# Dense SwiGLU: two thirds of the gate and up blocks as 2 by 2 block products with seven multiplications

## The chip, the core and the metric

The kernel runs on one core of a Trainium2 chip. The metric is the device time of one execution in microseconds. TensorE multiplies (PE in the profile; PEld is its weight load), VectorE (DVE), ScalarE (ACT) and GpSimd (POOL) do elementwise work, and SyncE (SP) issues nearly all of the transfers from device memory. Each engine works through its own instructions in a fixed order.

## The reference

The program is a two-layer encoder trunk on 512 tokens of width 1024. The part that matters here is the dense feed-forward stage at the end of the first layer:

```python
def swiglu(h, wg, wu, wd):
    return (jax.nn.silu(h @ wg) * (h @ wu)) @ wd
# h = rms_norm(x, norm_ffn[l]) is 512 x 1024; wg, wu are 1024 x 2816; wd is 2816 x 1024
x = x + swiglu(h, ffn_wg[j], ffn_wu[j], ffn_wd[j])
```

All of it is float32. The second layer has a mixture of experts in this place, which the change does not touch.

## The kernel before

Each float32 operand is split into two float16 parts, a high part and a low rest, and a product takes three float16 passes: high by high, low by high, high by low (`passes`). An activation is stored transposed, as eight tiles of 128 rows by 512 tokens for each part (`fh`, `fl`).

`ffn` first normalises x and transposes it (`norm_T`), row tile by row tile. Then it walks over 22 column blocks f of 128 columns. For each block it needs gate and up, so two weight blocks of 1024 x 128. `wtile` loads a block (`raw`, 512 KB), ACT writes the high part (`whi`, L266) and DVE the low part (`wlo`, L271). `proj_feat` then makes 24 matmuls of 512 columns into one PSUM bank (`pf`, L289). The first block goes through `proj_first` (L301), which takes the tokens in two halves of 256 columns so that it can start before all four row tiles are normalised. After gate and up, ACT applies silu, DVE multiplies, and the result is split into `uh` and `ul`. At the end `resid` multiplies by `wd` (L331) and adds to x.

Weight tiles come from a pool with two `raw`, three `whi` and three `wlo` buffers; a load is issued by SP when its buffer is free, and SP issues in a fixed order. PSUM gives the stage four banks for products (`acc`) and four for transposes (`sm`). A scheduler fixes the order of each engine's instructions when the program is built. The first weight blocks are loaded and split long before the stage, during the memory attention.

Of the kernel before, what the change touches and what calls it, by code (L numbers as in the profile page):

```python
# [8 lines left out]
F32 = mybir.dt.float32  # L9
# [18 lines left out]
SW = 64.0  # L28
# [26 lines left out]
class Kern:  # L55
# [151 lines left out]
    @staticmethod  # L207
    def plain(t):
        return t.bitcast(F32) if t.dtype == F32R else t
# [1035 lines left out]
            output(1, 1)  # L1245


    def ffn(self, l, x):
        nc, I, tc = self.nc, self.I, self.tc
        hh = self.hp.tile([P, KT, SEQ], F16, name="fh", tag="hh", bufs=1)  # L1250
        hl = self.hp.tile([P, KT, SEQ], F16, name="fl", tag="hl", bufs=1)
        self.norm_T(x, NT, [(I["norm_ffn"][l], hh, hl)])
        j = l // 2
        FT = 22
        hk, lk = [hh[:, k, :] for k in range(KT)], [hl[:, k, :] for k in range(KT)]
        with tc.tile_pool(name="ffn", bufs=1, reuse_waits="tile") as fp:
            uh = fp.tile([P, FT, SEQ], F16, name="uh")
            ul = fp.tile([P, FT, SEQ], F16, name="ul")
            for f in range(FT):
                fs = slice(f * P, (f + 1) * P)  # L1260
                ws = [I["ffn_wg"][j][:, fs], I["ffn_wu"][j][:, fs]]
                if f == 0:
                    pg, pu = self.proj_first(ws, hk, lk)
                else:
                    pg, pu = (self.proj_feat(w, hk, lk) for w in ws)
                s = fp.tile([P, SEQ], F32, name="fs", bufs=2)
                nc.scalar.activation(s, pg, AF.Silu, scale=1 / SW)
                nc.vector.scalar_tensor_tensor(s, pu, 0.125 / SW, s, OP.mult, OP.mult)
                self.split_ps(uh[:, f, :], ul[:, f, :], s)
# [535 lines left out]
```

## Time and profile before

| | us |
|---|---|
| median of 3 runs (2078.53 to 2082.65) | 2080.55 |
| the profiled execution | 2075.39 |
| its span, from first to last instruction | 2073.6 |
| first product of the stage to its last gate or up product | 664.8 to 896.4 |
| `wd` products of the stage | 896.4 to 1008.8 |

In the profile, "busy" is the time in which an engine had an instruction in work, and a row of the chain of waits is a piece of the work that ended last. Matmuls are pipelined: the length of one record is longer than the distance to the next, so the rate is read from a run of many.

### The profile page before, as it was taken

To read this page: it belongs to the slowest core of one execution; us is meant where nothing else is said; L and a number is where in the kernel's file an instruction comes from. 1 tells how busy PE (TensorE), PEld (TensorE's weight loads), DVE (VectorE), ACT (ScalarE), POOL (GpSimd) and SP (SyncE) were. 2 spreads that over 40 slices of the span, in tenths; PEclk is the share of its full clock that TensorE was granted. 3 is DMA by queue.
4 is the path that set the end of the run, shared out by engine and by line. 5 is a ranking of instruction groups with operands and counts; after the bars stand their busy time and mean duration, and the time that the engine had idled before them with its cause. 6 is when DMAs were issued, how large, how long until landed. Compare 5 with 4: busy or idle time off the path is not lost.

```text
span 2073.6 us, 40817 instructions
## 1 busy us (share of the span) xinstructions
PE 1940.1 (94%) x16760; PEld 1286.0 (62%) x16760; DVE 1413.4 (68%) x2373; ACT 1029.1 (50%) x1661; POOL 341.0 (16%) x357
## 2 busy tenths in 40 slices
PE   6998899899898999999998989979998899999997
PEld 3764565465465444444574546537455799999996
DVE  6766987756676333322466998574757888888886
ACT  5543446453453333322443435544335678888883
POOL 2260611003010000000243260100201310000002
PEclk9998999979999999999999999988999899999998
DMA  7334334325642333333434342434535699999993
GB/s 234 106 80 99 87 90 127 97 64 159 221 147 62 102 102 102 102 102 102 121 81 94 89 120 65 120 99 130 173 114 202 189 394 365 356 355 347 345 344 127
DMA packets 346742, 332.52 MB, mean 160 GB/s; under 512 B 101921, under 2 KB 263841, under 8 KB 346546
## 3 DMA queue, kind: packets, MB, share of 16 engines
q1 hardware_dynamic: 335440, 306.03, 47.2%
q10 hardware_dynamic: 8482, 15.39, 2.0%
q0 software_dynamic: 2624, 8.40, 1.2%
q8 instruction: 133, 2.18, 0.4%
q14 instruction: 63, 0.52, 0.1%
HBM read 297.05 MB, written 32.72 MB: 159 GB/s over the span
## 4 chain that ended last, share of the span: by engine, by line
PE 70%; DVE 12%; DMA 7%; ACT 3%; issue 3%; POOL 3%; SPq 2%; DVEq 0%; ACTq 0%; POOLq 0%
PE pf L289 23%; PE ptok L331 12%; PE pe L1567 10%; PE py L1612 6%; PE pSy L904 3%; PE pf L301 3%; PE ptok L349 2%; PE psc L527 1%; DVE wlo L271 1%; DMA eraw<-in_moe_wd_dram 1%; DVE iacc L518 1%; DVE pr L1003 1%; PE pA L808 1%; PE pT L193 1%; PE pp L558 1%
## 5 line engine op out<-in xcount | busy, mean ns | idle before, releaser
L266 ACT ACTIVATE whi<-raw 128x1024 f16<-128x1024 f32 (+2 forms) x244 | 227.7, 934 | 436.9 <-PE pf L289 187.3
L271 DVE SCALAR_TENSOR_TENSOR wlo<-raw,whi 128x1024 f16<-128x1024 f32 (+2 forms) x210 | 232.0, 1107 | 201.7 <-ACT whi L266 190.3
L1550 DVE SCALAR_TENSOR_TENSOR ewlo<-eraw,ewhi 128x1024 f16<-128x1024 f32 x265 | 321.1, 1220 | 58.0 <-ACT ewhi L1549 56.7
L289 PEld LDWEIGHTS <-whi 128*128 128x128 f16 x1888 | 182.5, 99 | 229.5 <-issue 34.8
L1549 ACT ACTIVATE ewhi<-eraw 128x1024 f16<-128x1024 f32 x265 | 277.4, 1054 | 77.9 <-PE py L1612 34.6
L1567 PE MATMUL pe<-XT,ewhi 128*128 128x144 f16 x2816 | 206.3, 226 | 1.7 <-issue 1.7
L1567 PEld LDWEIGHTS <-ewhi 128*128 128x128 f16 x2816 | 183.4, 98 | 2.3 <-issue 1.6
L289 PE MATMUL pf<-hh,whi 128*128 128x512 f16 x448 | 171.7, 383 | 2.6 <-DVE v L613 1.0
L289 PE MATMUL pf<-hl,whi 128*128 128x512 f16 x448 | 171.5, 383 | 0.0
L289 PEld LDWEIGHTS <-wlo 128*128 128x128 f16 x944 | 92.4, 99 | 112.0 <-issue 9.0
L269 POOL TENSOR_TENSOR wlo<-raw,whi 128x1024 f16<-128x1024 f32 (+3 forms) x34 | 59.9, 1761 | 596.1 <-ACT raw L268 512.9
L289 PE MATMUL pf<-fh,whi 128*128 128x512 f16 x336 | 127.3, 379 | 0.0
L289 PE MATMUL pf<-fl,whi 128*128 128x512 f16 x336 | 127.3, 379 | 0.0
L1567 PE MATMUL pe<-XT,ewlo 128*128 128x144 f16 x1408 | 117.2, 226 | 0.1
L289 PE MATMUL pf<-hh,wlo 128*128 128x512 f16 x448 | 112.6, 386 | 0.0
L1612 PE MATMUL py<-HT,ewhi 128*128 128x144 f16 x1408 | 103.9, 227 | 0.1
L1567 PEld LDWEIGHTS <-ewlo 128*128 128x128 f16 x1408 | 94.3, 98 | 0.8 <-issue 0.7
L1612 PEld LDWEIGHTS <-ewhi 128*128 128x128 f16 x1408 | 92.5, 98 | 0.3 <-issue 0.2
L289 PE MATMUL pf<-fh,wlo 128*128 128x512 f16 x336 | 79.4, 379 | 0.0
L349 PE MATMUL ptok<-whi,hh 128*128 128x256 f16 (+1 forms) x320 | 74.7, 274 | 2.1 <-ACT qe L485 2.0
L349 PE MATMUL ptok<-whi,hl 128*128 128x256 f16 (+1 forms) x320 | 75.0, 274 | 0.0
L349 PEld LDWEIGHTS <-hh 128*128 128x128 f16 x640 | 62.4, 100 | 15.5 <-issue 8.2
(462 smaller groups left out, 3879.3 us busy)
## 6 DMA issues: line engine op xcount, KB each, us to landing
raw<-in_w_in_dram SPq DMA_DIRECT2D x76, 512.0 KB, 4.0
eraw<-in_moe_wg_dram SPq DMA_DIRECT2D x16, 2048.0 KB, 12.9
eraw<-in_moe_wu_dram SPq DMA_DIRECT2D x16, 2048.0 KB, 14.3
eraw<-in_moe_wd_dram SPq DMA_DIRECT2D x16, 2048.0 KB, 12.9
eraw<-in_moe_wg_dram SPq DMA_DIRECT2D x8, 1536.0 KB, 11.9
eraw<-in_moe_wu_dram SPq DMA_DIRECT2D x8, 1536.0 KB, 14.6
eraw<-in_moe_wd_dram SPq DMA_DIRECT2D x8, 1536.0 KB, 8.5
raw<-in_ffn_wg_dram SPq DMA_DIRECT2D x22, 512.0 KB
```

The lines of the kernel that those rows point to most:

```text
L266: nc.scalar.activation(hi, raw, AF.Copy, scale=SW)
L269: nc.gpsimd.tensor_tensor(lo, raw, hi, OP.subtract)
L271: nc.vector.scalar_tensor_tensor(lo, raw, SW, hi, OP.mult, OP.subtract)
L289: self.nc.tensor.matmul(p, lhsT=w[:, k, :], rhs=x[k], start=first, stop=last)
L301: m = self.nc.tensor.matmul(ps[i][:, cs], lhsT=w[:, k, :], rhs=x[k][:, cs], start=hf == 0 and start, stop=stop, skip_group_check=True)
L331: mm(ps[t][:, :N], lhsT=x[:, k0 + k, ts], rhs=w[:, k, :], start=k0 == 0 and first, stop=k0 + kg == kt and last)
L349: mm(p, lhsT=x[:, k0 + k, ts], rhs=w[:, k, :], start=k0 == 0 and t % 2 == 0 and first, stop=k0 + kg == kt and last, skip_group_check=True)
L904: m = mm(p[e][:, cc % 4, jj, :], lhsT=l, rhs=r, start=first[e] is None, stop=x == (1 if cc else 0), skip_group_check=True)
L1549: a = nc.scalar.activation(r[0], w, AF.Copy, scale=SW)
L1550: d = nc.vector.scalar_tensor_tensor(r[1], w, SW, r[0], OP.mult, OP.subtract)
L1567: mm(p[:, i * n:(i + 1) * n], lhsT=w[:, k, :], rhs=XT[:, k, h, :], start=z == 0, stop=z == len(ms) - 1)
L1612: mm(ps[d], lhsT=w[:, i, d * P:(d + 1) * P], rhs=HT[:, k, h, :], start=k == 0 and w is wh and h == 0 and d % per == 0, stop=k == FT - 1 an ...
```

## The change

Fourteen of the 22 blocks (all f that are not divisible by 3) are computed by `seven`. There gate and up together are one product of a 512 x 1024 by a 1024 x 256 matrix, seen as 2 by 2 blocks: two halves of the tokens, two halves of the 1024 rows, and gate and up as the two column halves. The Winograd form needs seven block products where the plain way needs eight. Each block product is 12 matmuls of 256 columns.

For this, sums of the activation blocks (S1 to S4) are formed once, in `sums_seven`, from the normalised row tiles, transposed and split. Sums of the weight blocks (T1 to T4, in `sTa` and `sTb`) are formed for each f by four subtractions on POOL. ACT and DVE split B11 with B21, B22, T1 with T2, and T3 with T4 into high and low parts. The results are combined by three copies on ACT and four additions on DVE. Both gate and up of such a block are loaded into a new tile `sraw` (two buffers). The pairs of `sTa` and `sTb` have one buffer each, the split parts two. f = 0, 3, 6, ... 21 stay plain and keep the old weight pool.

```diff
-        self.norm_T(x, NT, [(I["norm_ffn"][l], hh, hl)])
...
+            with tc.tile_pool(name="ffns", bufs=1, side="right", reuse_waits="tile") as sp:
+                xs = self.norm_T(x, NT, [(I["norm_ffn"][l], hh, hl)], None, sp)
+                plain(0, *self.proj_first(blocks(0), hk, lk))
+                self.sums_seven(sp, [t.rearrange("p (a b) -> p a b", a=2) for t in xs], ops)
+            with tc.tile_pool(name="ffn", bufs=2, reuse_waits="tile") as fp:
+                for f in range(1, FT):
+                    if f % 3:
+                        self.seven(fp, *blocks(f), ops, uh[:, f, :], ul[:, f, :])
+                    else:
+                        plain(f, *[self.proj_feat(w, hk, lk) for w in blocks(f)])
...
+    def seven(self, fp, wg, wu, ops, uh, ul):
...
+        raw = fp.tile([P, KT, 256], F32, name="sraw")
+        for i, w in enumerate((wg, wu)):
+            nc.sync.dma_start(raw[:, :, i * P:(i + 1) * P], w.rearrange("(k p) c -> p k c", p=P))
...
+        sub(Ta[:, 0], B(0, 1), B(0, 0))
+        sub(Tb[:, 0], B(1, 1), B(0, 1))
+        sub(Ta[:, 1], B(1, 1), Ta[:, 0])
+        sub(Tb[:, 1], B(1, 0), Ta[:, 1])
...
+            nc.scalar.activation(hi, src, AF.Copy, scale=SW)
+            nc.vector.scalar_tensor_tensor(lo, src, SW, hi, OP.mult, OP.subtract)
...
+        prod(a, 0, "A11", "B11")
+        nc.scalar.copy(p1, a[:, 0])
+        prod(a, 1, "A12", "B21")
+        prod(b, 0, "S3", "T3")
+        nc.scalar.copy(p7, b[:, 0])
+        prod(b, 1, "S1", "T1")
+        nc.vector.tensor_tensor(v, b[:, 1], p7, OP.add)
+        nc.vector.tensor_tensor(R[:, 0], a[:, 1], p1, OP.add)
+        prod(a, 0, "S2", "T2", True)
+        nc.scalar.copy(u2, a[:, 0])
+        nc.vector.tensor_tensor(R[:, 3], a[:, 0], v, OP.add)
+        prod(b, 0, "A22", "T4", True)
+        prod(b, 1, "S4", "B22", True)
+        nc.vector.tensor_tensor(R[:, 1:3], b, u2[:, None, :].to_broadcast([P, 2, 256]), OP.add)
```

The new order on SP, before and after the change, at the start of the stage. Before, the loads that follow the gain vector `gb0` are, one by one, the remaining plain blocks (up of f = 2, gate of f = 3, and on):

```order
L247 DMA gb0_9105<-in_norm_mix_dram 128x1024
L259 DMA raw_7092<-in_ffn_wu_dram 128x8x128
L259 DMA raw_7128<-in_ffn_wg_dram 128x8x128
L259 DMA raw_7159<-in_ffn_wu_dram 128x8x128
L259 DMA raw_7195<-in_ffn_wg_dram 128x8x128
```

After the change, the loads that were issued early belong to f = 0, f = 3 and the gate of f = 6. Behind `gb0` come the up of f = 6 (`raw_7691`) and the gate of f = 9 (`raw_7983`), and only then the four loads of f = 1 (`sraw_7081`) and f = 2 (`sraw_7209`):

```order
L247 DMA gb0_6803<-in_norm_ffn_dram 128x1024
L259 DMA raw_7691<-in_ffn_wu_dram 128x8x128
L259 DMA raw_7983<-in_ffn_wg_dram 128x8x128
L1305 DMA sraw_7081<-in_ffn_wg_dram 128x8x128
L1305 DMA sraw_7081<-in_ffn_wu_dram 128x8x128
L1305 DMA sraw_7209<-in_ffn_wg_dram 128x8x128
L1305 DMA sraw_7209<-in_ffn_wu_dram 128x8x128
```

So f = 1 and f = 2, which the old order had loaded before the stage, now stand behind two loads of later blocks.

The order on ACT, at the same place, after the change. `whi_7662` is the high part of the gate of f = 6; `sB11h`, `sB22h`, `sT1h` and `sT3h` are the high parts for f = 1 (7090 to 7102) and f = 2 (7218, 7222); `sp1_7108` is the copy of the first block product of f = 1:

```order
L266 ACTIVATE whi_7662<-raw_7660 128x1024
L201 CAST s3h_6793<-pT_7034 128x4x128
L201 CAST uh_6795<-fs_7000 128x512
...
L1318 ACTIVATE sB11h_7090<-sraw_7081 128x1024
L1318 ACTIVATE sB22h_7094<-sraw_7081 128x512
L1318 ACTIVATE sB11h_7218<-sraw_7209 128x1024
L1339 COPY sp1_7108<-pf_7106 128x256
L1318 ACTIVATE sB22h_7222<-sraw_7209 128x512
L1318 ACTIVATE sT1h_7098<-sTa_7084 128x1024
L1318 ACTIVATE sT3h_7102<-sTb_7085 128x1024
```

The copy and the splits of T1 and T3 for f = 1 have moved behind work that needs the loads of f = 2. The program makes the second product of f = 1 wait for that copy, since both are in one PSUM bank.

The order on DVE there, after the change (`wlo_7663` is the low part of the gate of f = 6, which frees the buffer for `raw_7983`; the rows ending in l are the low parts of f = 1 and f = 2):

```order
L271 SCALAR_TENSOR_TENSOR wlo_7663<-raw_7660,whi_7662 128x1024
...
L1319 SCALAR_TENSOR_TENSOR sB11l_7091<-sraw_7081,sB11h_7090 128x1024
L1319 SCALAR_TENSOR_TENSOR sB22l_7095<-sraw_7081,sB22h_7094 128x512
L1319 SCALAR_TENSOR_TENSOR sB11l_7219<-sraw_7209,sB11h_7218 128x1024
L1319 SCALAR_TENSOR_TENSOR sB22l_7223<-sraw_7209,sB22h_7222 128x512
L1319 SCALAR_TENSOR_TENSOR sT1l_7099<-sTa_7084,sT1h_7098 128x1024
```

Each of these has two operands in SBUF, and POOL makes the four subtractions of f = 1 in the same stretch.

## Rows read from the trace of the kernel before

**Rows 1.** Page, part 1: engine, busy us, share of span, instructions.

```profile
PE 1940.1 (94%) x16760; PEld 1286.0 (62%) x16760; DVE 1413.4 (68%) x2373; ACT 1029.1 (50%) x1661; POOL 341.0 (16%) x357
```

**Rows 2.** Windows: busy time of each engine, granted clock, DMA share, GB/s.

```profile
660.00:682.00 22.00, 19.89 (x146) 15.34 (x145) 12.62 (x18) 10.02 (x16) 1.66 (x3) 0.92 0.08 26
682.00:720.00 38.00, 38.00 (x177) 17.21 (x176) 14.13 (x16) 13.44 (x17) 0.00 (x0) 1.00 0.43 124
...
1700.00:1750.00 50.00, 50.00 (x786) 49.82 (x784) 42.61 (x44) 40.20 (x50) 2.44 (x2) 1.00 1.02 381
```

**Rows 3.** Chain of waits in order of time: start, length, work.

```profile
670.20 0.87 PE pT L193 x8
...
677.64 3.27 PE pf L301 x30
680.91 215.62 PE pf L289 x999
896.53 112.25 PE ptok L331 x520
```

**Rows 4.** Groups of instructions, 682 to 895 us: busy, mean ns, idle before.

```profile
L271 DVE SCALAR_TENSOR_TENSOR wlo<-raw,whi 128x1024 f16<-128x1024 f32 x42 | 51.2, 1220 | 56.7 <-ACT whi L266 56.7
L266 ACT ACTIVATE whi<-raw 128x1024 f16<-128x1024 f32 x43 | 45.4, 1056 | 102.0 <-PE pf L289 100.1 <-DMA raw<-in_ffn_wu_dram 1.9
...
L202 DVE TENSOR_TENSOR ul<-fs,uh 128x512 f16<-128x512 f32 x21 | 14.4, 685 | 0.0
L201 ACT CAST uh<-fs 128x512 f16<-128x512 f32 x21 | 13.0, 619 | 28.3 <-DVE fs L1268 28.3
```

**Rows 5.** Timeline, 679.5 to 684 us: start, length, engine, instruction.

```profile
679.53 1.22 DVE L271 SCALAR_TENSOR_TENSOR wlo<-raw,whi 128x1024 f16<-128x1024 f32 x1 [4.98 <-ACT whi L266]
...
679.88 1.04 PE L301 MATMUL pf<-fh,wlo 128*128 128x256 f16 x8
...
681.30 1.05 ACT L266 ACTIVATE whi<-raw 128x1024 f16<-128x1024 f32 x1
...
682.38 1.22 DVE L271 SCALAR_TENSOR_TENSOR wlo<-raw,whi 128x1024 f16<-128x1024 f32 x1 [0.26 <-ACT whi L266]
...
683.63 0.38 SPq L259 DMA_DIRECT2D raw<-in_ffn_wg_dram  x1
```

**Rows 6.** Transfer issues: tile, queue, count, size, us to landing.

```profile
raw<-in_ffn_wu_dram SPq DMA_DIRECT2D x22, 512.0 KB, 3.8
```

**Rows 7.** Groups of instructions on POOL, whole span.

```profile
L1075 POOL TENSOR_TENSOR mf<-mf,tb 128x512 f32<-128x512 f32 x16 | 23.7, 1488 | 28.7 <-DVE tb L1074 28.7
...
L269 POOL TENSOR_TENSOR wlo<-raw,whi 128x512 f16<-128x512 f32 x4 | 4.6, 1154 | 5.9 <-ACT raw L268 5.9
```

**Rows 8.** Timeline, two places where DVE and POOL meet.

```profile
485.31 0.69 DVE L271 SCALAR_TENSOR_TENSOR wlo<-raw,whi 128x512 f16<-128x512 f32 x1
485.47 1.65 POOL L1075 TENSOR_TENSOR mf<-mf,tb 128x512 f32<-128x512 f32 x1 [6.16 <-DVE tb L1074]
...
496.67 1.15 POOL L269 TENSOR_TENSOR wlo<-raw,whi 128x512 f16<-128x512 f32 x1
496.74 1.64 DVE L936 TENSOR_TENSOR yc<-yc,var 128x512 f32<-128x512 f32 x1 [1.17 <-POOL var L165]
```

**Rows 9.** Groups of instructions with 256 elements, DVE and ACT.

```profile
L271 DVE SCALAR_TENSOR_TENSOR wlo<-raw,whi 128x256 f16<-128x256 f32 x24 | 10.8, 452 | 1.1 <-ACT whi L266 0.8
...
L869 ACT COPY H<-pH 128x256 f32<-128x256 f32 x16 | 5.2, 375 | 6.1 <-PE pH L866 6.0
```

**Rows 10.** Timeline, 665.9 to 667.5 us: matmuls of 256 columns.

```profile
665.95 0.42 PE L301 MATMUL pf<-fl,whi 128*128 128x256 f16 x1
666.16 0.42 PE L301 MATMUL pf<-fh,whi 128*128 128x256 f16 x1
...
667.09 0.27 PE L301 MATMUL pf<-fl,whi 128*128 128x256 f16 x1
667.20 0.27 PE L301 MATMUL pf<-fh,whi 128*128 128x256 f16 x1
```

More of the change, by code (lines that the diff above doesn't have):

```diff
@@ L1255, in ffn @@
         hk, lk = [hh[:, k, :] for k in range(KT)], [hl[:, k, :] for k in range(KT)]
[L1256 to L1269, printed above, removed]
-            self.resid(I["ffn_wd"][j], uh, ul, x, FT, 8.0)
+        ops = {n: tuple(h[:, 4 * q:4 * q + 4, i * 256:(i + 1) * 256] for h in (hh, hl))
+               for n, i, q in (("A11", 0, 0), ("A12", 0, 1), ("A22", 1, 1))}
@@ new lines, in ffn, with plain @@
+        with tc.tile_pool(name="ffnx", bufs=1, reuse_waits="tile") as xp:
+            for i in range(4):
+                ops[f"S{i + 1}"] = tuple(xp.tile([P, 4, 256], F16, name=f"s{i}{c}") for c in "hl")
+            uh = xp.tile([P, FT, SEQ], F16, name="uh")
+            ul = xp.tile([P, FT, SEQ], F16, name="ul")
+            blocks = lambda f: [I[w][j][:, f * P:(f + 1) * P] for w in ("ffn_wg", "ffn_wu")]
+            def plain(f, pg, pu):
+                t = xp.tile([P, SEQ], F32, name="fs", bufs=2)
+                nc.scalar.activation(t, pg, AF.Silu, scale=1 / SW)
+                nc.vector.scalar_tensor_tensor(t, pu, 0.125 / SW, t, OP.mult, OP.mult)
+                self.split_ps(uh[:, f, :], ul[:, f, :], t)
+            with tc.tile_pool(name="ffns", bufs=1, side="right", reuse_waits="tile") as sp:
[8 more added lines that the diff above has]
+                        plain(f, *[self.proj_feat(w, hk, lk) for w in blocks(f)])
+            self.resid(I["ffn_wd"][j], uh, ul, x, FT, 8.0)
@@ new lines, in sums_seven @@
+    def sums_seven(self, sp, xs, ops):
+        nc = self.nc
+        for tt in range(2):
+            x0, x1 = xs[tt], xs[2 + tt]
+            S = [sp.tile([P, 512], F32, name=f"S{i}") for i in range(4)]
+            nc.gpsimd.tensor_tensor(S[2], x0[:, 0, :], x1[:, 0, :], OP.subtract)
+            nc.vector.tensor_tensor(S[0], x1[:, 0, :], x1[:, 1, :], OP.add)
+            nc.vector.tensor_tensor(S[1], S[0], x0[:, 0, :], OP.subtract)
+            nc.vector.tensor_tensor(S[3], x0[:, 1, :], S[1], OP.subtract)
+            for i in (2, 0, 1, 3):
+                p = self.sm("pT")
+                for k in range(4):
+                    nc.tensor.transpose(p[:, k * P:(k + 1) * P], S[i][:, k * P:(k + 1) * P], self.ident)
+                self.split_ps(*[o[:, :, tt * P:(tt + 1) * P] for o in ops[f"S{i + 1}"]], p.rearrange("p (k t) -> p k t", k=4))
```

29 lines of the change are left out of this document (added).

## The prediction

> **What bounds the kernel now.** I read part 1 of the page first: PE is busy for 94% of the span, DVE for 68%, POOL for 16% [rows 1]. That is an average, so I cut the windows to the stage that changes. From 682 us on PE is busy for all of its 38 us, at full granted clock, while DVE is busy for 14.1 us, ACT for 13.4 and POOL for nothing [rows 2]. The chain of waits says the same more strictly: from 680.91 us there are 215.62 us of nothing but gate and up products, 999 matmuls, and the `wd` products follow at 896.53 without a break [rows 3]. So here the stage lasts as long as its matmuls, 215.62/999 = 0.2158 us for one of 512 columns. A plain block has 48 of them: 10.36 us. Every other engine only has to keep up.
>
> **What the seven products save.** A block by `seven` has 7 x 12 = 84 matmuls of 256 columns. The first block of the stage already runs in such halves: 30 of them take 3.27 us of the chain, 0.109 each, each with its own weight load [rows 3]. So a block costs 84 x 0.109 = 9.16 us and saves 1.20. Fourteen blocks save **16.8 us**, if PE never waits. (Were the price 0.125 instead, 84 of them would cost 10.5 us and the saving would be gone; the 30 in a row say it is not.)
>
> **What is added on PE before the stage flows.** The sums S1 to S4 need 8 groups of 4 transposes. Eight transposes take 0.87 us [rows 3], so a group takes 0.43. In the new order three groups stand before the last product of f = 0 (+1.3 us) and five behind it (2.2 us, inside the wait below). The transposes of the third row tile now also stand ahead of nearly all of the first half of f = 0, and they wait for two more DVE splits of 0.69 us [rows 4]. I take +1.0 for that, between 0 (the second half, which needs the fourth row tile, had room) and 2.5.
>
> **The start, where the saving goes.** Before, eight products of f = 1 of 0.216 us (1.9 us) were already worked in before f = 0 was done, and its weights lay ready. In the new order f = 1 needs `sraw_7081`, and its load stands on SP behind the gate of f = 9 (`raw_7983`), which waits until the gate of f = 6 is split into both parts. The old trace shows the same wait: the last products of f = 0 begin at 679.88 and cover about 0.9 us, the high part of the next block is made from 681.30, the low part from 682.38, and SP issues at 683.63 [rows 5]. That is 3.0 us after the last product, which I call T0 (before: 680.64). T0 itself goes to 680.64 - 1.9 + 1.3 + 1.0, about 681.0.
>
> From T0 + 3.0 SP issues five loads of 512 KB, 0.4 us apart (0.38 in the row). One lands 3.8 us after its issue [rows 6]. Behind one another they cannot land closer than 512 KB by the rate: 124 GB/s at a share of 0.43 is 288 GB/s for all engines, 1.8 us; the expert stage reaches 381 GB/s, 1.4 us [rows 2]. I take 1.6. Landings: `raw_7983` at T0 + 6.8, gate and up of f = 1 at 8.4 and 10.0, of f = 2 at 11.6 and 13.2. Now step by step with 1.06 us for a split of 1024 on ACT, 0.6 for 512, 1.22 and 0.69 on DVE [rows 4], 0.37 for a copy of 256 [rows 9]:
> - ACT makes B11 and B21 of f = 1 from 8.4 to 9.5; PE starts its first product at 9.5. It was idle from 2.2 on.
> - The second product waits for the copy of the first, and that stands on ACT behind B11 and B21 of f = 2 (11.6 to 12.7): 13.1.
> - The third needs T3, so all four subtractions on POOL, from 10.0 on. POOL takes 1.15 us for 512 elements with a float16 result and 1.49 on average in the group with float32 [rows 7]. I take 1.2 for the work and count the waits apart. Laid end to end that is 10.0 + 4.8 = 14.8. ACT has B22 of f = 2 in front (13.2 to 13.8), then T1 (to 14.9) and T3 (to 16.0), so the third product could start at 16.0.
>
> **Where DVE and POOL meet.** They don't run side by side when both read two operands from SBUF. At 485.31 DVE splits a tile for 0.69 us, POOL starts at 485.47 and takes 1.65, which is the rest of DVE's instruction and then some 1.12; at 496.67 POOL goes first with its 1.15, and DVE's product, 0.69 by its size, takes 1.64 and ends 0.56 after POOL [rows 8]. Each waits out the other's whole instruction. In the new order the four subtractions share their stretch with four low parts on DVE, one after the other: B11 of f = 1 (to 10.7), subtraction (11.9), B22 (12.6), subtraction (13.8), B11 of f = 2 (15.0), subtraction (16.2), B22 of f = 2 (16.9), subtraction (18.1). Then T3 on ACT: the third product starts at T0 + 19.2, not 16.0.
>
> The Trainium skill has a rule for this and it speaks against the change: the page "SBUF — State Buffer", section "Who interferes with whom", says that a DVE instruction with two SBUF inputs and a GpSimd instruction that reads SBUF take one shared port pair in turn, each holding it for its whole length. By that rule the third product starts at 19.2, without it at 16.0, and the sum would be 3.2 us less; the rows above agree with the rule.
>
> Until then PE has done 24 of the matmuls of 0.109, 2.6 us of work (at the half clock that follows idle time, 0.21 apart instead of 0.11 [rows 10], but it waits anyway). The start so costs 19.2 - 2.6 = **16.6 us**, between 12.5 (loads 1.4 apart, no meeting on the port) and 18.5 (1.8 apart, subtractions of 1.49).
>
> **What follows the start.** A group of three blocks takes PE 2 x 9.16 + 10.36 = 28.7 us. DVE has in it eight instructions of 1.22, ten of 0.69 and six of 0.45 [rows 4, 9], 19.4 us. Those with two SBUF operands (eight of 1.22, seven of 0.69) and eight subtractions of 1.2 add to 24.2 us that must go in turn. That fits, but only 4.5 us in 28.7 are free to win back a late start. The subtractions of f = 2 can't begin before the T1 of f = 1 is split, since `sTa` has one buffer; they end near T0 + 26, and T3 of f = 2 near 27.5, when PE has just run out (19.2 + 60 x 0.109 = 25.7, and one product more). The next pair follows behind the same queues. I put 5 us on these later waits, and on the clock if it falls again: 0 if all is caught up at once, 10 if two pairs lose 5 us each.
>
> **The sum**, against the profiled execution of 2075.39 us: -16.8 + 1.3 + 1.0 + 16.6 + 5.0 = +7.1, so 2082.5. (The 1.9 us of work done early is in T0.) That execution was 5.2 us below the median of the runs shown; with the same difference the median goes to 2080.55 + 7.1 = **2087.7 us**. Nothing behind 896 us changes, as the `wd` loads and products keep their order.
>
> **The rivals.** About 0.2%, 4.2 us, is what a measurement here tells from no change.
> - No change, 27%: DVE and POOL do not hold each other up here, the third product starts at 16.0, the start costs 13.4, and only 1.5 is lost later. -16.8 + 1.3 + 1.0 + 13.4 + 1.5 = +0.4: 2081.0. For it: the rows of the meeting are few, and DVE is busy for little over a third now. Against it: every low part here has two SBUF operands.
> - Faster, 10%: the loads land as a single one does, at 3.8 each, so the subtractions begin at T0 + 7.6, and the third product starts at 13.3; loss 10.7. -16.8 + 10.7 + 1.3 + 0.5 = -4.3: 2076.2. It decides from a loss under 10.6. Against it: five loads follow each other within 1.6 us.
> - Slower through the whole stage, 13%: each subtraction takes the 1.49 of the long rows and holds up DVE as long. 19.4 + 8 x 1.49 = 31.3 us in a group of 28.7; six further groups lose 2.6 each, 15.6 beside the 7.1: 2103. It decides from about 1.2 us for a subtraction if DVE is then never free beside it. Against it: nine of DVE's 24 instructions in a group read one of their operands from PSUM and can run beside POOL.
>
> **How the numbers follow.** The forecast, slower by 7 through the start, has 50%. Its own range, with the bounds above not all at one end, is 2079 to 2095. Reaching into the rivals until 2 in 10 are left out gives 2077.5 to 2098. Chances: faster by over 0.2% 0.10; within 0.2% 0.28 (the second case, and a little of the first); slower 0.62.
>
> **What would show it.** PE should idle some 7 us after f = 0, then wait twice more within f = 1, for a copy and for T3 on ACT; SP should issue the first `sraw` load about 3.4 us after the last product of f = 0. Steady pairs should run at 0.109 a matmul, the group near 28.7 us. POOL's subtractions should show lengths of 1.2 to 2.4 us where DVE is at a low part. I am wrong if the first block product starts before T0 + 8, if the later groups show no wait at all on PE, or if they take over 29.5 us each.

## The result and the profile after

| | us |
|---|---|
| kernel before, median of 6 runs | 2079.45 |
| changed kernel, median of 6 runs (2094.78 to 2106.47) | 2097.98 |
| ratio, 95% interval | 1.0095, 1.0073 to 1.0117 |
| profiled execution of the changed kernel, its span | 2106.47, 2104.6 |

The change makes the kernel slower by some 18.5 us, where +7.1 was forecast: 10 us over the forecast of 2087.7, outside its own range (2079 to 2095) and at the very end of the wider one (2077.5 to 2098). Each ratio here and below is taken over all runs with its interval, so it need not be the quotient of the two medians. The profiled execution is the slowest of the six. Part 1 of the page of the changed kernel, against [rows 1]:

```profile
PE 1939.6 (92%) x17296; PEld 1344.5 (64%) x17296; DVE 1506.3 (72%) x2471; ACT 1070.0 (51%) x1739; POOL 437.9 (21%) x415
```

TensorE has as much busy time as before, in a longer span. Windows of the stage (length, busy time of PE, PEld, DVE, ACT and POOL, granted clock, DMA share, GB/s), against [rows 2]:

```profile
660.00:682.00 22.00, 18.09 (x156) 15.82 (x156) 19.14 (x30) 13.62 (x24) 5.16 (x5) 1.00 0.09 27
682.00:700.00 18.00, 8.06 (x49) 5.80 (x50) 12.93 (x12) 6.54 (x9) 10.06 (x6) 0.75 0.73 193
700.00:730.00 30.00, 28.95 (x209) 20.59 (x208) 27.25 (x23) 15.40 (x22) 25.71 (x15) 0.98 0.42 115
730.00:760.00 30.00, 28.56 (x200) 20.29 (x200) 22.37 (x25) 15.12 (x23) 12.91 (x8) 0.94 0.34 93
760.00:880.00 120.00, 120.00 (x915) 89.18 (x913) 90.80 (x101) 62.02 (x92) 45.62 (x28) 1.00 0.36 100
```

TensorE is idle for 3.9 us up to 682 (2.1 before the change), for 10 between 682 and 700, for 2.5 up to 760, and not at all from there to 880. The timeline of the changed kernel at the marks that matter (start, length, engine, instruction, in brackets the idle time before it and what ended it); tiles `qhl` open the memory attention ahead of the stage, `fh` the stage, `uh` with `wlo` at 1014.91 is the last `wd` product, `tt` and `Bt` belong to layer 1's chunk inverse (`rwkv_inverse`):

```profile
574.90 1.49 PE L301 MATMUL pf<-qhl,whi 128*128 128x256 f16 x6
...
663.75 0.38 PE L301 MATMUL pf<-fh,whi 128*128 128x256 f16 x2 [0.24 <-ACT fh L201]
...
677.00 1.04 PE L301 MATMUL pf<-fh,wlo 128*128 128x256 f16 x8
...
681.18 0.58 SPq L1305 DMA_DIRECT2D sraw<-in_ffn_wg_dram  x1
...
686.65 1.06 ACT L1318 ACTIVATE sB11h<-sraw 128x1024 f16<-128x1024 f32 x1 [3.32 <-DMA sraw<-in_ffn_wg_dram]
...
687.76 0.40 PE L1329 MATMUL pf<-fh,sB11h 128*128 128x256 f16 x1 [5.05 <-ACT sB11h L1318]
...
691.64 0.27 PE L1329 MATMUL pf<-fh,sB11h 128*128 128x256 f16 x1 [1.14 <-ACT sp L1339]
...
696.78 0.28 PE L1329 MATMUL pf<-s2h,sT3h 128*128 128x256 f16 x1 [3.67 <-ACT sT3h L1318]
...
774.88 0.27 PE L1329 MATMUL pf<-s0h,sT1h 128*128 128x256 f16 x1
...
803.58 0.27 PE L1329 MATMUL pf<-s0h,sT1h 128*128 128x256 f16 x1
...
901.38 0.38 PE L331 MATMUL ptok<-whi,uh 128*128 128x512 f16 x1
...
1014.91 0.59 PE L331 MATMUL ptok<-wlo,uh 128*128 128x512 f16 x2
...
1366.32 0.16 DVE L986 TENSOR_TENSOR pr<-tt,Bt 128x1 f32<-128x1 f32 x1 [6.41 <-DMA Bt<-scrA]
...
1387.11 0.54 DVE L986 TENSOR_TENSOR pr<-tt,Bt 128x225 f32<-128x225 f32 x1
```

From the first `fh` product to the first `wd` product it takes 901.38 - 663.75 = 237.6 us; before, 231.5 (664.85 to 896.37, rounded in the table ahead of the prediction; 669.00 to 900.46 below). So the stage costs 6.1 us, and most of the 18.5 is elsewhere. The same marks of the kernel before, from a second profile of it (run e12 below):

```profile
575.13 1.27 PE L301 MATMUL pf<-qhl,whi 128*128 128x256 f16 x5
...
638.23 0.18 DVE L594 TENSOR_SCALAR mu<-mu 128x14 f32<-128x14 f32 x1 [3.33 <-DMA mu<-in_rwkv_mu_dram]
...
669.00 0.61 PE L301 MATMUL pf<-fh,whi 128*128 128x256 f16 x2
...
900.46 0.38 PE L331 MATMUL ptok<-whi,uh 128*128 128x512 f16 x1
...
1013.99 0.59 PE L331 MATMUL ptok<-wlo,uh 128*128 128x512 f16 x2
...
1352.68 0.16 DVE L986 TENSOR_TENSOR pr<-tt,Bt 128x1 f32<-128x1 f32 x1 [5.19 <-DMA Bt<-scrA]
...
1365.08 0.55 DVE L986 TENSOR_TENSOR pr<-tt,Bt 128x225 f32<-128x225 f32 x1
```

The 15-step recursion of the inverse takes 12.4 us here from its first step to its last product, 20.8 in the changed kernel, and it begins 338 us behind the last `wd` product here and 351 there. No line of that code is changed. Its order is: this is VectorE's order around the twelfth step, in the kernel before and then in the changed one (`mf` is a gate product, `s` a score, `wlo` and `ybl` low parts, each of other work in the layer):

```
L987 TENSOR_REDUCE tt<-pr 128x11
L986 TENSOR_TENSOR pr<-tt,Bt 128x144
L987 TENSOR_REDUCE tt<-pr 128x12
L986 TENSOR_TENSOR pr<-tt,Bt 128x169

L987 TENSOR_REDUCE tt<-pr 128x11
L541 ISA s,mx<-psc,mask 128x512
L541 ISA mx 128x1
L986 TENSOR_TENSOR pr<-tt,Bt 128x144
L205 SCALAR_TENSOR_TENSOR ybl<-po,ybh 128x256
L541 ISA s,mx<-psc,mask 128x512
L541 ISA mx 128x1
L987 TENSOR_REDUCE tt<-pr 128x12
L1063 SCALAR_TENSOR_TENSOR mf<-gt,pf 128x512
L271 SCALAR_TENSOR_TENSOR wlo<-raw,whi 128x256
L986 TENSOR_TENSOR pr<-tt,Bt 128x169
```

The scheduler that orders the engines when the program is built has put layer 1 together in another way, since the stage ahead of it is another one. Behind the `wd` loads 448 of VectorE's 1237 instructions stand at another place than before, 1762 of TensorE's 10047 and 122 of SyncE's 338.

### The profile page after: what moved, and what is told of

Same layout as the page of the kernel before. It is cut to its first block, busy times and chain, and to the rows that moved or that the text cites. A ratio compares the mean times of both kernels' runs of the same rounds, so it can differ in the third digit from the quotient of the medians.

```text
span 2104.6 us, 42184 instructions
## 1 busy us (share of the span) xinstructions
PE 1939.6 (92%) x17296; PEld 1344.5 (64%) x17296; DVE 1506.3 (72%) x2471; ACT 1070.0 (51%) x1739; POOL 437.9 (21%) x415
## 5 line engine op out<-in xcount | busy, mean ns | idle before, releaser
L266 ACT ACTIVATE whi<-raw 128x1024 f16<-128x1024 f32 (+2 forms) x216 | 198.0, 918 | 323.4 <-PE ptok L331 114.5
L271 DVE SCALAR_TENSOR_TENSOR wlo<-raw,whi 128x1024 f16<-128x1024 f32 (+2 forms) x182 | 197.4, 1086 | 136.5 <-ACT whi L266 122.8
L289 PEld LDWEIGHTS <-whi 128*128 128x128 f16 x1440 | 139.1, 99 | 175.7 <-issue 36.5
L289 PEld LDWEIGHTS <-wlo 128*128 128x128 f16 x720 | 70.0, 99 | 86.7 <-issue 10.3
L349 PEld LDWEIGHTS <-hh 128*128 128x128 f16 x640 | 62.3, 100 | 13.3 <-issue 5.9
L331 PE MATMUL ptok<-whi,uh 128*128 128x512 f16 x176 | 66.7, 379 | 0.0
L331 PE MATMUL ptok<-whi,ul 128*128 128x512 f16 x176 | 66.7, 379 | 0.0
L1697 PE MATMUL py<-HT,ewlo 128*128 128x144 f16 x704 | 59.2, 227 | 3.2 <-DVE ewlo L1635 3.2
## 6 DMA issues: line engine op xcount, KB each, us to landing
eraw<-in_moe_wu_dram SPq DMA_DIRECT2D x8, 1536.0 KB, 11.1
```

The source lines that it names most:

```text
L266: nc.scalar.activation(hi, raw, AF.Copy, scale=SW)
L271: nc.vector.scalar_tensor_tensor(lo, raw, SW, hi, OP.mult, OP.subtract)
L289: self.nc.tensor.matmul(p, lhsT=w[:, k, :], rhs=x[k], start=first, stop=last)
L331: mm(ps[t][:, :N], lhsT=x[:, k0 + k, ts], rhs=w[:, k, :], start=k0 == 0 and first, stop=k0 + kg == kt and last)
L349: mm(p, lhsT=x[:, k0 + k, ts], rhs=w[:, k, :], start=k0 == 0 and t % 2 == 0 and first, stop=k0 + kg == kt and last, skip_group_check=True)
L1697: mm(ps[d], lhsT=w[:, i, d * P:(d + 1) * P], rhs=HT[:, k, h, :], start=k == 0 and w is wh and h == 0 and d % per == 0, stop=k == FT - 1 an ...
```

## The experiments

The first question was whether that order, or something else behind the stage, costs the time. A table (`ROWS`) holds for each engine the order of one built kernel's instructions, and the other kernel is given issue-order edges along it, which add no waits.

**e1 and e2: the block products in the old order, and the plain blocks in the new one.** e1 is the changed kernel with the rows of the kernel before, from the first `wd` load on; e2 the kernel before with the rows of the changed one.

```diff
+    def pin(self):
+        ins = self.nc.cur_bb.bb.instructions[self.n0:]
+        base = int(ins[0].name[2:])
+        by = {int(i.name[2:]) - base: i for i in ins}
+        for row in zlib.decompress(base64.b85decode(ROWS)).decode().split("\n"):
+            seq = list(itertools.accumulate(map(int, row.split())))
+            for a, b in zip(seq, seq[1:]):
+                self.order(by[b], by[a])
...
+                self.pin()
                 self.overflow(j, ovf, hd, x, slot, gate, out)
```

> The changed kernel, in which everything from the wd product of layer 0 to the end of the program stands, on every engine, in the very order that it has in the kernel before (a table of issue-order edges without waits pins it); the block products are as in the changed kernel. Theory O (order): of the +31.0 us of the changed kernel's profiled span only about +6.1 arises in the SwiGLU stage (norm product 664.8 before, 663.7 after; wd 896.4 before, 901.4 after), and the rest because the instructions of layer 1 stand in another order on all engines; so here layer 1 takes what it takes before, and the median is 2079.5 + 6.1 = 2085.6 us (2082 to 2090). Theory H (hardware): the order is harmless and layer 1 runs slower after this stage for another reason (clock, other addresses, or the run): the time stays near 2098 (2094 to 2102), and layer 1 again loses its 20 us between about 1210 and 1500 us.

> The kernel before, untouched in its 22 plain column blocks, but with everything from the wd product of layer 0 on in the order that it has in the changed kernel. Theory O: layer 1 loses here what it loses in the changed kernel; 2098.0 - 6.1 = 2092 us (2088 to 2100), without a single block product. Theory H: the time stays at 2079.5 (2077 to 2083).

**e3: the changed kernel again**, unedited.

> The changed kernel once more, beside the two others on the same chip. Both theories: median 2095 to 2101 us. Theory O: the stage takes again some 6 us more than before (from the first product of the norm's operands to the wd product), the rest of the difference lies behind 1210 us. If the profiled run's +31 was mostly a slow single run, the loss of layer 1 in this profile is nearer 13 us (18.5 of the medians less 6.1) than 25.

Against 2081.73 for the kernel before on that chip: e1 2086.04 (1.0030, 1.0017 to 1.0043), e2 2095.93 (1.0072, 1.0058 to 1.0087), e3 2101.09 (1.0091, 1.0074 to 1.0107). The plain kernel, with no block product in it, is 14 us slower in the new order, and the block products in the old order lose most of the excess. Theory O holds, theory H falls. That e1 came out so near the 2085.6 of its expectation is partly luck: its stage takes 243.1 us up to the first `wd` product and not 237.6, as the old order puts layer 1's small vectors ahead of the `wd` loads and TensorE waits 5.3 us there, and 4.7 us come back ahead of the stage (below).

**e12 and e13: the kernel before, and the block products with the old order behind `wd`, for more profiles.** (e13 repeats e8 below.)

> The kernel before itself, for a second profile beside the others. By segments (0 to the first product on the norm's operands, from there to the last wd product, the rest) the one profile there is has 664.9 + 345.4 + 1063.3; the profiles with the old order of layer 1 have 1061.5 to 1067 in the rest, those with the new one 1087.9 to 1089.5. Theory O: the rest is 1061 to 1068 here again. If it is 1070 or more, the first profile was a lucky one, and the order costs less than 24 us.

> The block products with the old order behind wd, a second time (2079.98, ratio 0.9996 with 0.9983 to 1.0008 in the first, where the stage was 6 us longer than in the kernel before and 1.002 to 1.004 was expected). If the 6 us of the stage count in full, the ratio is 1.002 to 1.004 here and the first was low by chance; if something else gives them back, 0.998 to 1.001 again, and the three segments say where.

e12 gave 2084.31 against 2081.95 (1.0003, 0.9980 to 1.0026), e13 2079.64 (0.9994, 0.9977 to 1.0011). Each profile can be cut at three marks: the first `qhl` product, the first `fh` product, the end of the last `wd` product. What lies between does not depend on where a run stands at 570 us, which differs by 3.8 us between the two profiles of the kernel before (571.4 and 575.1):

| | `qhl` to `fh` | `fh` to end of `wd` | rest |
|---|---|---|---|
| before, the two profiles | 93.5, 93.9 | 345.6, 345.6 | 1063.1, 1068.6 |
| changed kernel, the two profiles | 88.9, 88.8 | 351.8, 351.7 | 1089.1, 1087.5 |
| e2, plain in the new order | 88.8 | 345.0 | 1087.5 |
| e8 and e13, sevens, old order behind `wd` | 88.8, 88.9 | 351.8, 351.6 | 1065.2, 1068.2 |

The rest is 1087.5 to 1089.1 in all three profiles with the new order, 1061.2 to 1075.5 with a mean of 1067.3 in thirteen with the old one, whatever the stage: **+21 us by the order of layer 1**. Single profiles of the old order lie up to 14 us apart in this part, but the two groups do not meet. The stage is +6.1. And the memory attention ahead of it, which nothing in the change touches, is 4.8 us *shorter* in the changed kernel. Together -4.8 + 6.1 + 20.7 = +22.0, where the medians say +18.5 and +19.4. The row that points at the 4.8 is the `mu` row above: in the kernel before VectorE stands 3.3 us in the middle of the memory attention in front of a small vector of layer 1 that has just been issued.

**e16: only the small vectors moved, in the plain kernel.** Its `ROWS` hold the old order behind `wd`, and `VEC` names the 12 small loads of layer 1 and the 11 VectorE instructions on them.

```diff
+        pre = self.nc.cur_bb.bb.instructions[:self.n0]
+        last = {e: next(i for i in reversed(pre) if i.engine == e and "Tile" not in type(i).__name__) for e in {by[x].engine for x in VEC}}
+        for x in VEC:
+            self.order(by[x], last[by[x].engine])
```

> The kernel before with its 22 plain blocks and its order behind wd; moved are only layer 1's 12 small loads (mu, w0 and the like, the next norm's gain) and the 11 VectorE instructions on them, which now stand behind the SwiGLU stage, as they do in the changed kernel. In the two profiles of the kernel before VectorE stands 3.1 and 3.3 us in front of mu's load in the middle of the memory attention, and from the first qhl product to the first product on the norm's operands it takes 93.5 and 93.9 us; 88.8 to 88.9 in the kernels by seven products and in the plain one with the new order. Theory M (that wait is what the changed kernel gets back ahead of the stage): 88.8 here too, the rest as before, ratio 0.9970 to 0.9985 (4.7 us less). Rival N (the memory attention is faster for another reason, such as the norm's rows in tiles of their own): 93 to 94 again and ratio 0.999 to 1.001.

2076.71 against 2082.30: ratio 0.9972, 0.9959 to 0.9985. The timeline of e16 at the two marks:

```profile
568.84 1.46 PE L367 MATMUL pf<-qhl,whi 128*128 128x256 f16 x6
...
657.58 0.38 PE L367 MATMUL pf<-fh,whi 128*128 128x256 f16 x2 [0.24 <-ACT fh L267]
```

88.7 us: theory M holds for the vectors together; 3.3 of the 4.8 us are seen in the one wait. In the changed kernel SP issues them behind the stage (`mu` at 904.4 us, before at 630.0). Why the scheduler moved them was not tried; they stand behind the gain load of the next norm, which waits for a tile of the last block by seven (shown for e4 below).

**e14: VectorE's order alone.** The changed kernel with the `ROWS` of VectorE and no others.

> The changed kernel with the order of the kernel before on VectorE alone (its 1225 instructions behind the wd product); the other four engines as the scheduler puts them around that (539 of 10047 rows on TensorE and 29 of 338 on SyncE still differ, 1762 and 122 in the changed kernel). Theory V (VectorE's order makes the loss: the 15-step recursion of the chunk inverse took 13 us from its first step in the kernel before and 21 us in the changed one, since scores, splits and gate products stand between its steps): most of the 24 us come back, the time is within 4 us of the run with all engines pinned (2076 to 2085). Rival T (transfers: SyncE's new order of loads and of the inverse's round trips through memory, or TensorE's): half or more of the loss stays, 2088 or more.

2091.00 (1.0039, 1.0022 to 1.0057), rest 1074.9. The timeline of e14 at the inverse:

```profile
1357.34 0.16 DVE L1009 TENSOR_TENSOR pr<-tt,Bt 128x1 f32<-128x1 f32 x1 [4.54 <-DMA Bt<-scrA]
...
1369.74 0.55 DVE L1009 TENSOR_TENSOR pr<-tt,Bt 128x225 f32<-128x225 f32 x1
```

The recursion is back at 12.4 us, and it begins 343 us behind `wd` (1357.34 - 1014.4), where it is 349 to 351 in the three profiles with the new order and 334 to 339 in the thirteen with the old one. Neither theory is right alone, though the time is in rival T's range: 8 of the 21 us are VectorE's recursion torn apart, some 13 arise before it, and of those 5 to 11 stay when VectorE alone is put back (7.6 by the rest, 7 by the mean start of the recursion, 11.4 by the medians of e14 and e13). On which engine they hang was not tried.

**e4 to e7: where the stage's own 6 us go.** e4 is e1 with SyncE's rows only from behind its last `wd` load on.

> As the run with the block products and the old order of layer 1, but SyncE's first 34 transfers behind the SwiGLU stage (the wd loads and layer 1's small vectors) stand where the scheduler puts them; in the first such run the vectors stood ahead of wd and the wd product began 5.27 us late behind its load. It is the base of the next three. Theory O: that wait goes, the stage takes 237.6 us from the norm's first product to the wd product as in the changed kernel (243.1 in the first run), and the time is 0 to 3 us over that of the kernel before. If the order explains less than thought, 5 us or more over it.

2090.03 against 2082.22 (1.0041, 1.0026 to 1.0055): no gain. The waits of e4 on SyncE's queue from 850 to 930 us (engine, line, what it waited for, us in total, times, longest):

```profile
SPq L323 <- DVE wlo L335: 36.4, 8, 18.8
SPq L311 <- DVE sR L1416: 32.7, 1, 32.7
```

The load of the next norm's gain (L311) waits 32.7 us for a tile of the last block by seven, and with it all but two `wd` loads. This wait is one of my edit, not of the change, which has five `wd` loads ahead of it. TensorE waits 5.2 us for it at the start of `wd`. e5 to e7 are therefore compared with e4 alone (the base of their expectations), e5 and e7 by `fh` to the first `wd` product.

e5:

```diff
                         self.seven(fp, *blocks(f), ops, uh[:, f, :], ul[:, f, :])
+                        if f == 2:
+                            self.lasts = self.lastS
...
             self.lastw = nc.sync.dma_start(raw[:, :, o:o + n], pc.rearrange("(k p) c -> p k c", p=P)).ins
+            if self.lasts:
+                self.order(self.lastw, self.lasts)
```

> The base with one edit: the raw loads of the plain blocks f = 3 and later are issued behind the four block loads (sraw) of f = 1 and 2; now two of them (f = 3 wu, f = 6 wg) stand ahead in SyncE's queue and wait for buffers until VectorE has split f = 3's weights, so that the first sraw goes out at 677.4, 3.3 us after the last product of f = 0 (674.1 in the repeated run). Theory Q (the queue holds the start): POOL and ScalarE can begin some 10 us sooner, the first block product follows the S transposes at once, and PE's waits of 5.0 + 1.1 + 3.7 us between the transposes and T3 shrink to under 4; the time falls by 6 to 9 us. Theory D (VectorE and POOL hold it): VectorE is busy 19 of 22 us there anyway, so the splits of f = 1 come no sooner than 3 us before, and the time falls by 0 to 3 us.

2083.43 (1.0013, 0.9995 to 1.0030), 6.6 us less than e4; 232.4 us for the stage instead of 237.6. By the time theory Q, but not by the waits: TensorE's idle time from 650 to 730 is still 12.4 us, where e4 has 16.7, and 6.8 of it lie in five pieces between 682 and 700, four for VectorE's splits and sums and one of 1.9 for a copy on ACT. This is one of them, where VectorE and POOL meet (timeline of e5):

```profile
684.77 1.22 DVE L337 SCALAR_TENSOR_TENSOR wlo<-raw,whi 128x1024 f16<-128x1024 f32 x1
684.99 2.13 POOL L1379 TENSOR_TENSOR sTa<-sraw 128x512 f32<-128x512 f32 x1 [11.05 <-DVE sT1l L1390]
...
685.91 2.29 DVE L1390 SCALAR_TENSOR_TENSOR sT3l<-sTb,sT3h 128x1024 f16<-128x1024 f32 x1
...
687.20 2.13 POOL L1379 TENSOR_TENSOR sTa<-sraw,sTa 128x512 f32<-128x512 f32 x1
688.12 2.28 DVE L337 SCALAR_TENSOR_TENSOR wlo<-raw,whi 128x1024 f16<-128x1024 f32 x1
```

Each ends 1.07 to 1.13 us after the other has ended, so it does most of its work only then: alone, `wlo` takes 1.22 us and the shortest subtractions 1.27. Both theories hold in part.

e6:

```diff
-                    if f % 3:
+                    if f not in (1, 2, 5, 8, 11, 14, 17):
```

> The base with another choice of plain blocks: f = 0, 1, 2, 5, 8, 11, 14, 17 plain and the other 14 by seven products, so that two plain blocks (20.7 us of TensorE) stand between the S transposes and the first block product. Both theories of the start: the wait is covered either way; no wait over 1 us on the first block products, the time falls by 8 to 11 us against the base (clock included), to 6 to 9 us under the kernel before (ratio 0.996). If the four blocks by seven in a row at the end (f = 18 to 21) are held by VectorE, some 2 us come back there.

2080.13 (0.9994, 0.9976 to 1.0012), 9.9 us less than e4, within the 8 to 11 of both theories, but their detail was wrong: TensorE still waits 3.1 us for a copy and 1.8 for T3 at the first block products, and the time is not 6 to 9 us under the kernel before. At the start of `wd` it waits longer than in e4 (waits of e6 on TensorE from 880 to 930 us):

```profile
PE ptok L395 <- DVE wlo L335: 8.6, 1, 8.6
```

The first `wd` product is no mark here, as 48 products of the last block stand behind it (in e10 too).

e7:

```diff
-        Ta, Tb = (fp.tile([P, 2, 4, P], F32, name=n, bufs=1) for n in ("sTa", "sTb"))
-        sub = lambda o, a, b: nc.gpsimd.tensor_tensor(o, a, b, OP.subtract)
-        sub(Ta[:, 0], B(0, 1), B(0, 0))
...
+        Ta, Tb = raw[:, :, P:].rearrange("p (i k) c -> p i k c", i=2), raw[:, :, 0:P].rearrange("p (i k) c -> p i k c", i=2)
```

> The base without POOL's four subtractions a block (14 x 6.8 us of POOL): T1 to T4 are views of the raw blocks, so the sums of products are other ones; everything else (splits, products, loads) stays. Theory P (VectorE and POOL hold each other up, as in the prediction): the two large T splits on VectorE fall from 1.4 to 2.2 us to near 1.2 each, T3's first product of f = 1 comes 3 to 4 us sooner, the time falls by 3 to 5 us. Rival: only the load's landing counts at the start, and later nothing waits; the time falls by under 1.5 us.

With other values the router fills the experts differently and the part for overflow at the end runs (4446.6 us in all), so only the stage can be read: 226.6 us, 11.1 less than e4, far more than theory P's 3 to 5. Of that 7.2 is idle time of TensorE between 682 and 730 (9.5 in e4, 2.3 in e7); a granted clock of 0.85 from 682 to 700 and 1.00 from 730 to 760, where e4 has 0.75 and 0.96, goes with it. Groups on VectorE from 676 to 886 us (line, engine, operation, tiles, shapes, count, busy, mean ns, idle before), first of the changed kernel, then of e7:

```profile
L1319 DVE SCALAR_TENSOR_TENSOR sT3l<-sTb,sT3h 128x1024 f16<-128x1024 f32 x14 | 23.9, 1705 | 15.5 <-ACT sT3h L1318 15.4
...
L1354 DVE SCALAR_TENSOR_TENSOR fs<-sR,fs 128x512 f32<-128x512 f32 x12 | 19.9, 1661 | 0.2 <-ACT fs L1353 0.2
...
L1319 DVE SCALAR_TENSOR_TENSOR sB22l<-sraw,sB22h 128x512 f16<-128x512 f32 x14 | 17.6, 1255 | 0.2 <-ACT sB22h L1318 0.2
L271 DVE SCALAR_TENSOR_TENSOR wlo<-raw,whi 128x1024 f16<-128x1024 f32 x14 | 17.0, 1217 | 2.3 <-issue 1.5 <-ACT whi L266 0.7
...
L1351 DVE TENSOR_TENSOR sR<-pf,su 128x512 f32<-128x512 f32 x13 | 8.9, 681 | 1.8 <-PE pf L1329 1.8
```

```profile
L1379 DVE SCALAR_TENSOR_TENSOR sT3l<-sraw,sT3h 128x1024 f16<-128x1024 f32 x14 | 17.1, 1224 | 16.7 <-ACT sT3h L1378 16.7
...
L335 DVE SCALAR_TENSOR_TENSOR wlo<-raw,whi 128x1024 f16<-128x1024 f32 x12 | 14.6, 1221 | 3.4 <-issue 3.2 <-ACT whi L330 0.3
...
L1414 DVE SCALAR_TENSOR_TENSOR fs<-sR,fs 128x512 f32<-128x512 f32 x14 | 9.7, 692 | 3.1 <-ACT fs L1413 3.1
L1411 DVE TENSOR_TENSOR sR<-pf,su 128x512 f32<-128x512 f32 x14 | 9.6, 684 | 8.2 <-PE pf L1389 8.2
L1379 DVE SCALAR_TENSOR_TENSOR sB22l<-sraw,sB22h 128x512 f16<-128x512 f32 x14 | 9.5, 681 | 0.0
```

The block products' instructions with two operands in SBUF are shorter without POOL beside them, the last product `fs` by 1.0 us; the one that reads a bank of PSUM (`pf`) is not. The split of the plain blocks, `wlo`, has two such operands and is no shorter either: in the changed kernel five of its 14 meet a subtraction, all five began first and took 1.21 to 1.23 us, and it was the subtraction that took 1.86 to 2.07. POOL's groups in the changed kernel from 676 to 900 us, the longest and the shortest of the four:

```profile
L1308 POOL TENSOR_TENSOR sTa<-sraw,sTa 128x512 f32<-128x512 f32 x14 | 26.0, 1856 | 1.0
...
L1308 POOL TENSOR_TENSOR sTb<-sraw 128x512 f32<-128x512 f32 x14 | 21.3, 1521 | 6.9 <-DVE sT3l L1319 6.9
```

The shortest single one takes 1.26 us, and the one at 752.76, with VectorE idle, 1.27.

**e8 to e11: the change without its accident.** In e8 `ROWS` begin behind the `wd` product on every engine, so that the `wd` loads stand as in the changed kernel. It is "the first kernel of this call" in the expectations of e9 to e11, and e10 is "the run before it" in that of e11.

> The block products as in the changed kernel; only what follows the wd product (layer 1 and the experts) stands in the order that it has in the kernel before, the wd product itself is left to the scheduler, as in the changed kernel (five wd loads ahead of the next norm's gain and layer 1's vectors in SyncE's queue). In the runs before this one two wd loads or none stood ahead of that gain load, which waits for a tile of the last block by seven, and TensorE lost 5 to 10 us at the start of wd. Theory O: the stage costs +6 (237.6 us to the first wd product against 231.5), wd and layer 1 what they cost before; 1.002 to 1.004 of the kernel before, 2 to 6 us under the run with two wd loads ahead (2090.0). If layer 1 also needs its vectors early, it stays at 1.004.

2079.98 against 2081.67 (0.9996, 0.9983 to 1.0008). The table above has where the 6 us went that were expected: -4.8 in the memory attention, +6.1 in the stage.

e9 is e8 with the subtractions on VectorE:

```diff
-        sub = lambda o, a, b: nc.gpsimd.tensor_tensor(o, a, b, OP.subtract)
+        sub = lambda o, a, b: nc.vector.tensor_tensor(o, a, b, OP.subtract)
```

> As the first kernel of this call, with the four subtractions of a block on VectorE instead of POOL. Without any subtractions the stage was 11.1 us shorter (226.6 to the first wd product against 237.6), and VectorE busy 19.0 of 30 us in the steady part instead of 23.5. Theory P (POOL and VectorE hold each other up): a subtraction of 128x512 takes VectorE about 0.7 us (its other sums of that shape: 0.68), four 2.7 us against POOL's 6.8; VectorE's splits fall to 1.2 us each, it is busy some 24.5 of 30 us, T3 of f = 1 is there 3 to 5 us sooner, and the time falls by 3 to 7 us against the first kernel of this call. Rival V (VectorE alone bounds the start: it was busy 9.96 of 10 us there with the loads issued early): 5.4 us more work for f = 1 and 2 on it, and the time rises by 1 to 4 us.

2073.09 (0.9961, 0.9946 to 0.9977), 6.9 us less than e8, theory P's range. A subtraction takes VectorE 0.68 us where POOL took 1.52 to 1.86, and VectorE's splits are back at 1.22 (VectorE's groups of e9, same columns as above):

```profile
L1383 DVE SCALAR_TENSOR_TENSOR sT3l<-sTb,sT3h 128x1024 f16<-128x1024 f32 x14 | 17.1, 1220 | 7.7 <-ACT sT3h L1382 7.7
...
L1372 DVE TENSOR_TENSOR sTa<-sraw 128x512 f32<-128x512 f32 x14 | 9.6, 686 | 3.5 <-DMA sraw<-in_ffn_wu_dram 2.3 <-issue 1.2
```

The 6.9 us are not the price of the meeting alone. Alone, a subtraction takes POOL 1.27 us, so four in a row are 2.4 us shorter on VectorE even if nothing meets; the two shares were not measured apart. Nor does e9 hold the order ahead of `wd`: `qhl` to `fh` takes 87.5 us in it and 88.8 in e8. The stage up to the first `wd` product falls from 237.7 to 230.1.

e10 has e6's choice of blocks and the loads ahead; e11 both edits.

```diff
-                    if f % 3:
+                    if f not in (1, 2, 5, 8, 11, 14, 17):
...
+            for r in raws[:4]:
+                self.order(r, self.sraws[3])
             self.resid(I["ffn_wd"][j], uh, ul, x, FT, 8.0)
```

> As the first kernel of this call, with plain blocks f = 0, 1, 2, 5, 8, 11, 14, 17 and with the block loads of f = 3 and 4 ahead of the raw loads of f = 1 and 2 in SyncE's queue. TensorE's idle time from 650 to 730 us (16.7 us in the run with the wd loads free, 7.0 with three plain blocks first but late loads, 12.4 with early loads alone) falls to 2 to 4 us. Theory O, and the start as the only other cost: 10 to 13 us less than the first kernel of this call, 0.995 to 0.998 of the kernel before.

> The kernel with three plain blocks first and the early loads, and the subtractions on VectorE. Theory P: nothing waits at the start in either, so only what POOL takes from VectorE elsewhere is gained, mostly in the four blocks by seven in a row at the end (VectorE some 9.5 us a block with POOL's part, TensorE 9.16): 0 to 3 us less than the run before it. Rival V: VectorE has 9.9 us or more a block there, 1 to 3 us more.

e10 2068.93 (0.9938, 0.9922 to 0.9954), e11 2071.35 (0.9946, 0.9925 to 0.9967). Windows of e10:

```profile
650.00:690.00 40.00, 31.75 (x211) 21.52 (x210) 32.85 (x47) 23.39 (x37) 18.48 (x14) 0.91 0.19 53
690.00:730.00 40.00, 40.00 (x269) 26.10 (x268) 28.52 (x28) 19.64 (x27) 19.72 (x11) 1.00 0.47 132
```

TensorE does not wait from 690 on. The 8.2 us before that are mostly a wait of 5.5 for the weights of f = 1, whose loads now stand behind the block loads (in e11 7.85): not the 2 to 4 us expected. e11 is 2.4 us slower than e10, in rival V's range, but the intervals overlap, and the profiles have the difference in that wait at the start and not in the last four blocks. So where plain blocks cover the start, the move to VectorE gains nothing that can be seen.

**e15 and e17: the fastest version without any pin, and again with it.** e15 has e10's edits and no `ROWS`; e17 is e10 unedited.

> Three plain blocks first and the early block loads, without any pin: the scheduler places layer 1 as it likes. 393 of VectorE's 1237 rows stand elsewhere than in the kernel before. Theory O: its time is that of the pinned kernel (2068.9) plus what its own order of layer 1 happens to cost; 2070 to 2095, and the rest behind wd is longer than 1067 us if its inverse is torn apart too.

> The fastest version once more (three plain blocks first, early block loads, old order behind wd): 0.9938 with 0.9922 to 0.9954 in its first measurement. Sum from segments against the kernel before: memory attention 4.7 less, stage with wd 345.6 to 340.2, 5.4 less, the rest the same: 10.1 us less, 0.9951. Expected 0.993 to 0.996.

e15 2087.85 (1.0035, 1.0017 to 1.0053), rest 1083.1 us; e17 2071.99 (0.9948, 0.9933 to 0.9964). The same edits are 0.35% slower than the kernel before in the scheduler's order and 0.5% faster in the old one (0.6% in e10). Both changed builds drew a dearer layer 1 than the kernel before has. The theory's detail was wrong for e15: its recursion takes no longer than before (first step 1348.04, last product 1359.48), and the loss lies ahead of it: the first step stands 348.3 us behind the last `wd` product, where e12 has 338.1.

## Why the prediction was wrong

The step that failed is its last sentence on the sum: "Nothing behind 896 us changes, as the `wd` loads and products keep their order." The reason given covers the `wd` part alone, and there it holds (114.1 us in both, from the first product to the end of the last). But layer 1 behind it stands in another order on every engine and takes 21 us longer (e1 to e3, e8, e12 to e14). The same failed ahead of the stage, with the other sign: -4.8 us in the memory attention (e16). The orders of before and after were at hand, and I read them for the stage alone. The rest of the sum, term by term, with T0 at 677.8 (0.76 us behind the start of the last eight products of f = 0, as in the prediction):

- **The seven products, -16.8.** In the undisturbed stretch from 760 on a group of three blocks takes 803.58 - 774.88 = 28.70 us, as predicted. Right.
- **Transposes and norm, +2.3.** T0 lies 14.05 us behind the first `fh` product, before 15.8 with 1.9 of other work in it: +0.2, so this term was 2.1 us too large.
- **The start, +16.6.** The first `sraw` issue is 3.4 us behind T0 (predicted 3.4), the first block product 10.0 (9.5), the second 13.8 (13.1), the third 19.0 (19.2). Less 2.6 of work: 16.4. Right, and by the steps it named: the queue behind two plain loads (e5), then POOL and VectorE in turn (e7, e9).
- **Later waits, +5.0.** By subtraction 6.1 + 16.8 - 0.2 - 16.4 = 6.3; of it, 2.5 us of idle time from 700 to 760, a granted clock of 0.98 and 0.94 there (28.95 x 0.02 + 28.56 x 0.06 = 2.3 us) and products 0.21 instead of 0.11 us apart from 698 to 700 (1.0 us) are seen. So this term was 1.3 us too small.
- **The stage in sum: +7.1 predicted, +6.1 measured.** The two misses partly cancel, which is luck.

None of the prediction's three signs of being wrong came (the first block product at T0 + 10.0, later waits up to 746, 28.70 us a group). They all look at the stage, and none at what follows it.

The meeting of VectorE and POOL, which the prediction took from two places [rows 8], is shown now on whole groups: POOL's subtractions took 1.52 to 1.86 us on average (1.2 to 2.4 predicted) and VectorE's splits up to 1705 ns instead of 1224. The Trainium skill, page "SBUF — State Buffer", section "Who interferes with whom", gives the rule, including that a VectorE instruction with at most one SBUF input does not contend with GpSimd outside the 2-port perf modes; the groups of the changed kernel and of e7 agree with both halves, 1255 against 681 ns for two such operands and 681 against 684 for one. What the meeting costs the kernel was not measured by itself: without subtractions the stage is 11.1 us shorter (e7), with them on VectorE the kernel 6.9 (e8 to e9), of which a part is POOL's own slower pace. The prediction had 6.7 between its sum and the rival without a meeting; that this is so near the 6.9 is partly luck.

Of the rivals, "no change" had its mechanism refuted (e7, e9). "Faster" needed loads that land at 3.8 us each; ACT began the first split 5.5 us behind the issue (681.18 to 686.65), near the 5.0 of the sum. (Its third product comes at 7.6 + 4.8 + 1.06 = 13.5 and not at 13.3, which changes nothing.) "Slower through the whole stage" is excluded by 120.00 us of 120. The kernel did end up slower than all but that one, for a reason that no rival named.

## What to carry to other kernels

Where a scheduler orders the engines, a change in one stage is also a draw for every stage behind it and ahead of it: compare the orders of the whole program, and hold the rest fixed before judging the edit. Here the draw behind it (+21 us) was over three times the edit (+6), the one ahead of it -5, and with layer 1 held and the start rearranged an unpromising change became one that gains 0.5% (e10, e17). About half of that is not the block products' own: the plain kernel with the small vectors moved has 0.28% already (e16), and from `fh` to the end of `wd` e10 gains 5.4 us (345.6 to 340.2). For the edit itself: a product form with fewer matmuls pays once its sums and loads lie behind plain work, and elementwise work with two SBUF operands should not be put on POOL beside VectorE where VectorE also waits for its result (e9; with the start covered, e11 gains nothing by it).

## What the runs showed that I had not expected

- POOL's subtractions cost VectorE about as much as doing them there: without POOL a block's six large instructions take 5.7 us instead of 8.2 (the sum of the means of T3, T1, B11, B22, `fs` and `ul`: 1705 + 1431 + 1321 + 1255 + 1661 + 817 ns in the changed kernel, 1224 + 1220 + 1225 + 681 + 692 + 687 in e7), and four subtractions on VectorE are 2.7 us. POOL alone takes 1.27 us for one, VectorE 0.68.
- Layer 1's small vectors, issued early, cost the kernel before 4.8 us: VectorE works in order and waited 3.3 us for one of them, of 7 KB, in the middle of other work (e16, which moves all twelve, 0.9972).
- The kernel before itself varied from 2073.08 to 2092.42 us in e12's runs; its two profiles differ by 4 us up to 670 us and by 5.5 behind `wd`.
